# Weight splits of 1024 columns five steps ahead, and the decays moved beside the pair's own last projections, in a two-layer hybrid encoder on one Trainium2 core

## Chip, cores and metric

The kernel runs on one core of one Trainium2 chip. The metric is the device time of one execution in microseconds (us), median of several. Five engines work in their own queues, each strictly in order: PE (TensorE matmuls, with PEld for its weight loads), DVE (VectorE), ACT (ScalarE), POOL (GpSimd) and SP (SyncE, which here only issues transfers).

## What is computed

Two layers over 256 tokens of width 2048. Each projects the normalised input with one wide matrix, runs 16 heads of a bidirectional RWKV-7 scan beside 16 heads of windowed attention, gates both, and projects back onto the residual. Cut to what matters here:

```python
for l in range(DEPTH):
    h = rms_norm(x, norm_g[l])
    proj = jnp.einsum('btd,dc->btc', h, w_in[l])
    ...
    r, k, v, xw, xa = jnp.split(bidir_token_shift(rw_in, shift_mu[l]), rw_splits, axis=-1)
    y_rw = rwkv7_branch(r, k, v, xw, xa, ...)      # two scans, forward and backward
    y_at = window_attention(rope(q), rope(k_at), v_at, sink[l])
    mix = jnp.concatenate([y_rw * jax.nn.silu(g_rw), y_at * jax.nn.silu(g_at)], axis=-1)
    x = x + jnp.einsum('btc,cd->btd', mix, w_out[l])

# in rwkv7_branch, per direction d
w = -jax.nn.softplus(-(w0[d] + jnp.tanh(xw) @ decay_up[d])) - 0.5   # decays
a = jax.nn.sigmoid(a0[d] + xa @ iclr_up[d])                         # learning rates
```

`decay_up` and `iclr_up` have rank 96. With the row for w0, the decay tile has 97 rows.

## The kernel before

**Projections.** Every projection goes in column tiles of 128. A tile takes 16 steps (one per 128 rows of the contraction), and each step three matmuls of 256 columns (L286 to L288), since weights and inputs are held as a high and a low part: hi times XH, hi times XL, lo times XH. Weights come in halves of a tile, 128 x 1024, for 8 steps each: `wload` issues the transfer into raw (3 buffers), `wsplit` (L211) makes hi on ScalarE (L216) and lo = raw - hi on VectorE (L218), in two pieces of 512 columns, into rings of 2. A half's buffers are thus free again when PE has done the last step of the half before the one in progress. `Stream.run` walks the queue of all halves and lets the next half be loaded and split when `PREFETCH` = 2 steps of the present one are left.

**Windows.** The RWKV heads go in 8 pairs of heads per layer. After two tiles for xw and xa, pair p's four tiles (k, v, r and the gate gr, 16 steps each) fill window p: 64 steps in 14 slots of 4 or 5 steps. At the start of a slot the program puts small work of earlier pairs between the steps: `scan_p` of pair w-1 at the slots in STAGE_P (the elementwise preparation), `scan_i` of pairs w-2 and w-3 (inverts the in-chunk matrix, level by level: pq, QF, pd, tv, tt), `scan_b` of pairs w-3 and w-4 (walks the chunks: rh, suv, pcc, py). Windows 8 to 12 have the attention's projections and scores, then follow 16 tiles of the output projection. Windows 3 to 7 have all of this at once and are called steady here.

**Low-rank part.** At the first step of a pair's k tile `ups` issues two transfers into the ring g (2 buffers, L472): iup, 96 rows of 2 x 128, and dup, 97 rows of 2 x 128, for that pair. The ring g is shared with the gate's evacuation (`silu_evac`, L424 to L426), so SP can issue them only when the gate of the pair before is done (its last instruction writes vg). `value_evac` splits them into high and low parts after the v tile: iuh and duh on ScalarE (L455), iu and du on VectorE (L456), one buffer each. The first stage of `scan_p`, a window later, uses them in 12 matmuls (pza, L636 to L638), takes tanh of both halves (lw and th), and squares and scales k (t and kkr). The second adds 1 and runs two scans over lw. The third has the head sums of t (pk, L642), two exponentials and the reciprocal. The last sums km into pbn.

**Order.** PE runs in the order of the program. The other engines' instructions are ordered by a scheduler with priorities (lo gets 40, `scan_b` 95), so a split can run far from where it is written, as soon as the scheduler holds its operands for ready. PSUM pairs for the small work are a ring of 2.

Of the kernel before, what the change touches and what calls it, by code (L numbers as in the profile page):

```python
# [15 lines left out]
AF = mybir.ActivationFunctionType  # L16
# [5 lines left out]
T = 256  # L22
# [19 lines left out]


SLOTS = 14
STAGE_P = [4, 5, 6, 7, 8, 9, 10, 11, 13]
STAGE_I = (list(range(SLOTS)), [0, 1])
STAGE_B = (list(range(1, 14)), [1, 2, 3, 4])
ATT = [
# [3 lines left out]
]  # L52
PRIO_B = 95
PRIO_LO = 40
PREFETCH = 2


def _layout():
# [71 lines left out]
def hybrid_trunk_kernel(ctx, tc, xT, wi, wv, wo, par, fing, dup, iup, sink, pos, cst, out):  # L130
# [75 lines left out]
    def wload(src):  # L206
        raw = wrp.tile([128, 1024], F32, tag="raw", name="raw")
        SY.dma_start(out=raw, in_=src)
        return raw

    def wsplit(raw):  # L211
        hi = wsp.tile([128, 1024], F32R, tag="hi", name="hi")
        lo = wsp.tile([128, 1024], F32R, tag="lo", name="lo")
        for i in range(2):
            q = slice(i * 512, (i + 1) * 512)
            A.activation(hi[:, q], raw[:, q], AF.Copy)  # L216
            with tc.high_priority(offset=PRIO_LO):
                V.tensor_tensor(lo[:, q], raw[:, q], hi[:, q].bitcast(F32), op=ALU.subtract)  # L218
        return hi, lo

    def halves(src, first=None):
        return [lambda: wsplit(first if first is not None else wload(src[0])), lambda: wsplit(wload(src[1]))]

    class InTurn:

# [175 lines left out]
    def queue_inputs(l):  # L401
# [4 lines left out]
        def inproj(ct, evac, **kw):  # L406
            gemm(wi[l, ct], lambda: (L.XH, L.XL), evac, **kw)

        def shift_evac(j, place):
            def evac(pm):  # L410
                dst = place()
                u = st("u", [T], bufs=2)
                V.tensor_tensor(u, pm, L.norm.rb, op=ALU.mult)
                A.activation(dst, u, AF.Identity, scale=dpm(0, j))
                V.scalar_tensor_tensor(dst[:, 1:T], u[:, 0 : T - 1], prm(P_MU0, j), dst[:, 1:T], op0=ALU.mult, op1=ALU.add)
                V.scalar_tensor_tensor(dst[:, 0 : T - 1], u[:, 1:T], prm(P_MU1, j), dst[:, 0 : T - 1], op0=ALU.mult, op1=ALU.add)

            return evac
# [11 lines left out]
        def new(t, name, tag, bufs):  # L430
            def place():
                t[name] = st(tag, [T], bufs=bufs)
                return t[name]

            return place
# [37 lines left out]

            return begin

        def value_evac(p, t):
            ev = shift_evac(8 + p, new(t, "v", "vg", 8))

            def evac(pm):
                ev(pm)  # L480
                for n, rows in (("iu", RANK), ("du", RANK + 1)):
                    raw = t[n]
                    t[n] = (st(n + "h", [2, 128], F32R), st(n, [2, 128], F32R))
                    split(t[n], raw, rows)

            return evac

        for p, t in enumerate(L.ts):
            inproj(2 + 4 * p, shift_evac(p, new(t, "k", "kr", 4)), begin=ups(p, t))
            inproj(3 + 4 * p, value_evac(p, t))  # L490
            inproj(4 + 4 * p, shift_evac(16 + p, new(t, "r", "kr", 4)))
            inproj(5 + 4 * p, silu_evac(new(t, "gr", "vg", 8)))


# [125 lines left out]
    def layer(l):  # L620
# [22 lines left out]

        def scan_p(p, t):
            K, VV, R, iu, du = t["k"], t["v"], t["r"], t["iu"], t["du"]
            dd = lambda x: x.rearrange("p (d x) -> p d x", d=2)
            two = lambda x: x.unsqueeze(1).to_broadcast([128, 2, T])
            c8 = lambda x: x.rearrange("p (n j) -> p n j", j=64)  # L650

            pza = wpair("pza")
            pz, pa = pza[:, 0], pza[:, 1]
            for d in range(2):
                low_rank(pz[:, d * T : (d + 1) * T], [a[0 : RANK + 1, d, :] for a in du], [a[0 : RANK + 1] for a in L.TW])
            LW = st("lw", [2 * T])
            for d in range(2):
                low_rank(pa[:, d * T : (d + 1) * T], [a[0:RANK, d, :] for a in iu], [a[0:RANK] for a in L.XA])
            PA.activation(LW, pz, AF.Tanh, scale=0.5)
            TH = st("th", [2 * T])  # L660
            for d in range(2):
                PA.activation(TH[:, d * T : (d + 1) * T], pa[:, d * T : (d + 1) * T], AF.Tanh, scale=0.5, bias=dpm(NSH + 16, d * 8 + p))
            sq = st("t1", [T], bufs=3)
            PA.activation(sq, K, AF.Square, scale=prm(P_KK, p))
            KR = st("kkr", [T])
            PA.activation(KR, K, AF.Identity, scale=prm(P_KK, p))
            yield

            PV.tensor_scalar(LW, LW, 1.0, None, op0=ALU.add)
            msk = MSK.rearrange("p c j -> p (c j)")  # L670
            for x in (LW[:, 0:T], LW[:, T : 2 * T][:, ::-1]):
                PV.tensor_tensor_scan(x, msk, x, 0.0, op0=ALU.mult, op1=ALU.add)
            yield
            pk = wbank("pk")
            head_sums(pk, sq)
            PP = st("pp", [2, NC, 64])
            IP = st("ip", [2, NC, 64])
            PA.activation(PP.rearrange("p d c j -> p (d c j)"), LW, AF.Exp, scale=DECAY_C)
            PA.activation(IP.rearrange("p d c j -> p (d c j)"), LW, AF.Exp, scale=-DECAY_C)
            KD = st("kd", [T])  # L680
            PV.reciprocal(KD, pk[:, 0:T])
            PV.scalar_tensor_tensor(KD, KD, 1e24, KR, op0=ALU.min, op1=ALU.mult)
            yield

            MV = st("mv", [2, NC, 2, 64], bufs=3)
            BK = st("bk", [2, NC, 3, 64])
            km = st("lw", [2 * T])
            kr4 = KR.rearrange("p (c j) -> p c j", j=64)
            PV.scalar_tensor_tensor(MV[:, 0, :, 0, 1:64], PP[:, 0, :, 0:63], -1.0, kr4[:, :, 1:64], op0=ALU.mult, op1=ALU.mult)
            PV.scalar_tensor_tensor(MV[:, 1, :, 0, 0:63], PP[:, 1, :, 1:64], -1.0, kr4[:, :, 0:63], op0=ALU.mult, op1=ALU.mult)  # L690
            PA.activation(MV[:, 0, :, 0, 0:1], kr4[:, :, 0:1], AF.Copy, scale=-1.0)
            PA.activation(MV[:, 1, :, 0, 63:64], kr4[:, :, 63:64], AF.Copy, scale=-1.0)
# [261 lines left out]
        def scans(w):  # L954

            gens = []
            for lag, scan, at in ((4, scan_b, STAGE_B[1]), (3, scan_i, STAGE_I[1]), (3, scan_b, STAGE_B[0]), (2, scan_i, STAGE_I[0]), (1, scan_p, STAGE_P)):
                p = w - lag
                if 0 <= p < NP:
                    if (scan, p) not in chains:  # L960
                        chains[scan, p] = scan(p, L.ts[p])
                    gens.append((chains[scan, p], at))
            return gens
# [204 lines left out]
```

## Time and profile before

| | us |
|---|---|
| median of 3 runs | 1236.76 (1234.54 to 1237.37) |
| the profiled execution | 1234.27, span 1232.4 |
| PE busy | 1182.2 (96%) |
| VectorE busy | 930.7 (76%) |
| ScalarE busy | 743.0 (60%) |
| hi, 560 pieces of 512 | 328.1 busy, 625 ns each |
| lo, 560 pieces of 512 | 368.4 busy, 687 ns each |

The first part of the page gives each engine's busy time and share of the span. Group rows give line, engine, operation, output and inputs, shape and count, then busy time and mean, then the idle time of that engine just before and what ended it. A timeline row gives start, length, engine, line, operation, and in brackets the wait before it and its releaser. In a timeline an x2 row has merged two instructions.

### The profile page before, as it was taken

The page shows a single profiled execution, that of the slowest core. Times are in us where ns is not written, and L with a number is a line of the kernel's source. Part 1 is how long each engine was busy: PE and PEld are TensorE (multiplying, and loading weights), DVE is VectorE, ACT ScalarE, POOL GpSimd, SP SyncE. Part 2 cuts the span into 40 slices and gives each one's busy share as a digit, 9 for nine tenths or more (in the row PEclk, how much of TensorE's full clock was granted, in tenths as well). Part 3 has the DMA queues.
Part 4 walks back from the last instruction along what each step waited for, and adds up shares of the span by engine and source line. Part 5 has one row for each costly group of instructions (what it writes and reads, how often), then busy time and mean ns, then how long its engine had stood idle before and what let it go on. Part 6 is the DMA issues. An engine that isn't in the chain of part 4 may idle for free. (4 is left out here: it accounts for less than half of the span.)

```text
span 1232.4 us, 38183 instructions
## 1 busy us (share of the span) xinstructions
PE 1182.2 (96%) x16204; PEld 1096.3 (89%) x16204; DVE 930.7 (76%) x2067; ACT 743.0 (60%) x1838; POOL 19.1 (2%) x23
## 2 busy tenths in 40 slices
PE   6989999999999899999998999999999999999996
PEld 6978998999998889999998889999999888899996
DVE  7878778887876668856676788878887866786654
ACT  6546665766665567655555556675776565665553
POOL 0000000000000000000000000000000000000000
PEclk9999999999999999999999999999999999999998
DMA  7433333323323334467654333333323333445653
GB/s 249 157 136 116 105 117 109 105 96 114 119 89 99 117 112 144 140 214 240 209 182 147 124 128 93 106 111 111 105 94 106 124 102 127 131 130 178 211 192 121
DMA packets 60411, 166.72 MB, mean 135 GB/s; under 512 B 7728, under 2 KB 22736, under 8 KB 60240
## 3 DMA queue, kind: packets, MB, share of 16 engines
q1 hardware_dynamic: 60240, 164.27, 41.0%
q8 instruction: 127, 2.08, 0.7%
q14 instruction: 44, 0.36, 0.1%
HBM read 157.43 MB, written 4.19 MB: 131 GB/s over the span
## 5 line engine op out<-in xcount | busy, mean ns | idle before, releaser
L286 PE MATMUL pm<-XH,hi 128*128 128x256 f32 x1664 | 498.8, 300 | 9.4 <-ACT XH L179 5.9
L288 PE MATMUL pm<-XH,lo 128*128 128x256 f32 x1664 | 471.5, 283 | 4.8 <-DVE lo L218 4.6
L287 PE MATMUL pm<-XL,hi 128*128 128x256 f32 x1664 | 471.8, 284 | 0.1
L216 ACT ACTIVATE hi<-raw 128x512 fp32r<-128x512 f32 x560 | 328.1, 625 | 238.0 <-PE pm L287 147.9
L218 DVE TENSOR_TENSOR lo<-raw,hi 128x512 fp32r<-128x512 f32 x560 | 368.4, 687 | 96.7 <-ACT hi L216 89.2
L286 PEld LDWEIGHTS pm<-XH,hi 128*128 128x128 f32 x1664 | 317.3, 191 | 34.9 <-issue 13.0
L288 PEld LDWEIGHTS pm<-XH,lo 128*128 128x128 f32 x1664 | 318.3, 191 | 6.5 <-DVE lo L218 6.4
L287 PEld LDWEIGHTS pm<-XL,hi 128*128 128x128 f32 x1664 | 318.3, 191 | 0.9 <-DVE XL L180 0.9
L286 PE MATMUL pm<-MH,hi 128*128 128x256 f32 x512 | 144.1, 281 | 1.2 <-ACT hi L216 1.2
L288 PE MATMUL pm<-MH,lo 128*128 128x256 f32 x512 | 143.9, 281 | 0.4 <-DVE lo L218 0.4
L287 PE MATMUL pm<-ML,hi 128*128 128x256 f32 x512 | 143.8, 281 | 0.0
L286 PEld LDWEIGHTS pm<-MH,hi 128*128 128x128 f32 x512 | 96.6, 189 | 2.2 <-ACT hi L216 1.4
L288 PEld LDWEIGHTS pm<-MH,lo 128*128 128x128 f32 x512 | 96.6, 189 | 0.6 <-DVE lo L218 0.6
L287 PEld LDWEIGHTS pm<-ML,hi 128*128 128x128 f32 x512 | 96.6, 189 | 0.0
L908 ACT ACTIVATE suv<-pcc 64x128 f32<-64x128 f32 x128 | 34.2, 267 | 18.1 <-PE pq L835 11.8
L837 ACT ACTIVATE QF<-pq 128x256 f16<-128x256 f32 x80 | 30.8, 385 | 19.8 <-PE pq L835 19.0
L993 ACT ACTIVATE mv<-mv,mx 128x257 f32<-128x257 f32 x64 | 32.0, 503 | 17.5 <-DVE mx L990 17.3
L740 DVE TENSOR_TENSOR ge<-pg,C 128x1024 f32<-128x1024 f32 x32 | 39.1, 1221 | 3.2 <-PE pg L734 3.1
L844 DVE CAST_PREDICATED tv<-LV,pd 128x256 f16<-128x256 uint8 x80 | 34.4, 430 | 7.7 <-PE pd L843 6.9
L892 ACT ACTIVATE rh<-pcc 128x128 f32<-128x128 f32 x64 | 17.5, 273 | 35.4 <-PE pcc L890 35.0
L734 PE MATMUL pg<-mv,bk 64*128 64x128 f32 x512 | 37.2, 285 | 0.0
L845 DVE CAST_PREDICATED tt<-LV,pd 128x256 f16<-128x256 uint8 x80 | 34.1, 426 | 0.0
(239 smaller groups left out, 1845.8 us busy)
## 6 DMA issues: line engine op xcount, KB each, us to landing
raw<-wi SPq DMA_DIRECT2D x207, 512.0 KB, 3.3
raw<-wo SPq DMA_DIRECT2D x64, 512.0 KB, 4.3
raw<-wv SPq DMA_DIRECT2D x8, 512.0 KB, 3.3
rrot<-u SPq DMA_DIRECT2D x80, 32.0 KB, 2.0
vg<-xT SPq DMA_DIRECT2D x16, 128.0 KB, 4.6
xd<-vg SPq DMA_DIRECT2D x16, 128.0 KB, 2.4
vg<-xd SPq DMA_DIRECT2D x16, 128.0 KB, 3.3
g<-dup SPq DMA_DIRECT2D x16, 97.0 KB
```

The lines of the kernel that those rows point to most:

```text
L216: A.activation(hi[:, q], raw[:, q], AF.Copy)
L218: V.tensor_tensor(lo[:, q], raw[:, q], hi[:, q].bitcast(F32), op=ALU.subtract)
L286: PE.matmul(pm, wh, rh[:, kk, :], start=(kk == 0), stop=False)
L287: PE.matmul(pm, wh, rl[:, kk, :], start=False, stop=False)
L288: PE.matmul(pm, wl, rh[:, kk, :], start=False, stop=(kk == 15))
L734: PE.matmul(pg[:, h, c * 128 : (c + 1) * 128], BK[half[h], d, c, 1 - h : 3 - h, :].rearrange("p s j -> p (s j)"), MV[half[h], d, c].rearra ...
L740: V.tensor_tensor(GEd(d), pg.rearrange("p h (c x) -> p h c x", c=NC), gm[d].unsqueeze(1).unsqueeze(1).to_broadcast([128, 2, NC, 128]), op= ...
L837: A.activation(t_sub(QF), flat4(pq[:, :, 0:128]), AF.Copy)
L844: V.copy_predicated(t_sub(TC), t_mask, flat4(pd[:, :, 0:128]))
L845: V.copy_predicated(v_sub(TT), v_mask, flat4(pd[:, 0, 128:384].rearrange("p (d x) -> p d x", d=2)))
L908: A.activation(here(h), pc[half[h], 1], AF.Copy)
L993: A.activation(Sc[:, h, q, 0:257], Sc[:, h, q, 0:257], AF.Exp, scale=0.125, bias=mx[:, q : q + 1], accum_out=den[:, q : q + 1])
```

## The change

It does four things. (1) A weight half is split in one instruction of 1024 columns per engine (only the very first half keeps two pieces). (2) `PREFETCH` goes from 2 to 5. (3) The low-rank part of `scan_p` (12 matmuls, both tanh, the +1 and the two scans over lw) becomes `scan_d`, at slots 12 and 13 of the pair's own window; `scan_p` keeps nine stages, at slots 3 to 11 instead of 4 to 11 and 13. (4) The split of iup's and dup's tiles is written after the r tile instead of the v tile.

```diff
-STAGE_P = [4, 5, 6, 7, 8, 9, 10, 11, 13]
+STAGE_D = [12, 13]
+STAGE_P = [3, 4, 5, 6, 7, 8, 9, 10, 11]
...
-PREFETCH = 2
+PREFETCH = 5
...
-    def wsplit(raw):
+    def wsplit(raw, parts=1):
...
-        for i in range(2):
-            q = slice(i * 512, (i + 1) * 512)
+        for i in range(parts):
+            q = slice(i * 1024 // parts, (i + 1) * 1024 // parts)
             A.activation(hi[:, q], raw[:, q], AF.Copy)
...
-        return [lambda: wsplit(first if first is not None else wload(src[0])), lambda: wsplit(wload(src[1]))]
+        return [lambda: wsplit(first, 2) if first is not None else wsplit(wload(src[0])), lambda: wsplit(wload(src[1]))]
...
-        def value_evac(p, t):
-            ev = shift_evac(8 + p, new(t, "v", "vg", 8))
+        def receptance_evac(p, t):
+            ev = shift_evac(16 + p, new(t, "r", "kr", 4))
...
-            inproj(3 + 4 * p, value_evac(p, t))
-            inproj(4 + 4 * p, shift_evac(16 + p, new(t, "r", "kr", 4)))
+            inproj(3 + 4 * p, shift_evac(8 + p, new(t, "v", "vg", 8)))
+            inproj(4 + 4 * p, receptance_evac(p, t))
...
-        def scan_p(p, t):
-            K, VV, R, iu, du = t["k"], t["v"], t["r"], t["iu"], t["du"]
+        def scan_d(p, t):
+
+            iu, du = t["iu"], t["du"]
             pza = wpair("pza")
...
+            t.update(LW=LW, TH=TH)
+            yield
+
+            PV.tensor_scalar(LW, LW, 1.0, None, op0=ALU.add)
+            msk = MSK.rearrange("p c j -> p (c j)")
+            for x in (LW[:, 0:T], LW[:, T : 2 * T][:, ::-1]):
+                PV.tensor_tensor_scan(x, msk, x, 0.0, op0=ALU.mult, op1=ALU.add)
+            yield
+
+        def scan_p(p, t):
+            K, VV, R, LW, TH = t["k"], t["v"], t["r"], t["LW"], t["TH"]
...
-            for lag, scan, at in ((4, scan_b, STAGE_B[1]), (3, scan_i, STAGE_I[1]), (3, scan_b, STAGE_B[0]), (2, scan_i, STAGE_I[0]), (1, scan_p, STAGE_P)):
+            for lag, scan, at in ((4, scan_b, STAGE_B[1]), (3, scan_i, STAGE_I[1]), (3, scan_b, STAGE_B[0]), (2, scan_i, STAGE_I[0]), (1, scan_p, STAGE_P), (0, scan_d, STAGE_D)):
```

The order on the engines, at three places. In brackets stands what an instruction waits for: DMAHW is a transfer, PE, Activation (ScalarE) and DVE are engines. Lines of the changed kernel are 1 to 8 higher than those of before (L455 is L456 there, L890's rh is L900, L908 is L916).

ScalarE in window 6, from the copy of AB to the first tanh; duh and iuh (the high parts of dup's and iup's tiles for pair 6) are the third and second row from the end. Before:

```order
L231 ACTIVATE AB<-ge 64x512
L770 ACTIVATE bt<-pt 128x768 [waits PE_49]
L775 ACTIVATE suv<-pt 64x4x64 x4
L231 ACTIVATE MH<-t_4473 128x256
L216 ACTIVATE hi<-raw 128x512 [waits DMAHW0_49,PE_49,Activation_49]
L216 ACTIVATE hi<-raw 128x512
L414 ACTIVATE kr<-u,DP 128x256 [waits DVE_49]
L892 ACTIVATE rh<-pcc 128x128 [waits PE_49]
L837 ACTIVATE QF<-pq 128x2x64x2 [waits PE_49]
L455 ACTIVATE duh<-g 97x256 [waits DMAHW3_49,PE_49]
L455 ACTIVATE iuh<-g 96x256 [waits DMAHW2_49,PE_49]
L231 ACTIVATE lw<-pza 128x512 [waits PE_49]
```

The same window of the changed kernel, from the silu's tanh (g<-g) on:

```order
L426 ACTIVATE g<-g 128x256 [waits DVE_49]
L866 ACTIVATE q_4352<-pf 128x512 [waits PE_49]
L950 ACTIVATE t_4396<-py,PR 128x256 [waits PE_49]
L878 ACTIVATE vf<-pn 128x512 [waits PE_49]
L900 ACTIVATE rh<-pcc 128x128 [waits PE_49]
L456 ACTIVATE iuh<-g 96x256 [waits DMAHW2_49]
L456 ACTIVATE duh<-g 97x256 [waits DMAHW3_49]
L217 ACTIVATE hi<-raw 128x1024 [waits DMAHW7_49,PE_49,Activation_49]
L916 ACTIVATE suv<-pcc 64x2x64 [waits PE_49]
L916 ACTIVATE suv<-pcc 64x2x64
L232 ACTIVATE MH<-t_4396 128x256 [waits DVE_49]
L232 ACTIVATE AB<-ge 64x512 x2
```

The two splits moved from behind the second rh of the window to behind the first, ahead of suv, MH and AB, and no longer wait for PE.

VectorE at the start of the same window, from the gate's last instruction (vg) to the next lo; ge is the masked in-chunk matrix that AB is copied from, t the finished output of pair 2, whose high part is MH. Before:

```order
L426 SCALAR_TENSOR_TENSOR vg<-g 128x256 [waits Activation_49]
L804 COPY tv<-EYE 128x512 [waits PE_49]
L740 TENSOR_TENSOR ge<-pg,C 128x2x512 [waits PE_49]
L231 TENSOR_TENSOR t_4473<-t_4473,bv 128x256 [waits Activation_49]
L804 COPY tt<-EYE 128x512 [waits PE_49]
L231 SCALAR_TENSOR_TENSOR t_4473<-t_4473,vg 128x256 [waits DVE_49]
L740 TENSOR_TENSOR ge<-pg,C 128x2x512 [waits PE_49]
L218 TENSOR_TENSOR lo<-raw,hi 128x512 [waits DMAHW7_49,PE_49,Activation_49]
```

The changed kernel, from the gate's first instruction (g<-pm):

```order
L425 TENSOR_TENSOR g<-pm,rb 128x256 [waits PE_49]
L232 SCALAR_TENSOR_TENSOR lw<-MSK,lw 128x256 [waits DVE_49]
L232 SCALAR_TENSOR_TENSOR lw<-MSK,lw 128x256
L219 TENSOR_TENSOR lo<-raw,hi 128x1024 [waits DMAHW6_49,Activation_49]
L427 SCALAR_TENSOR_TENSOR vg<-g 128x256 [waits Activation_49]
L812 COPY tv<-EYE 128x512 [waits PE_49]
L748 TENSOR_TENSOR ge<-pg,C 128x2x512 [waits PE_49]
L812 COPY tt<-EYE 128x512 [waits PE_49]
L457 TENSOR_TENSOR iu<-g,iuh 96x256 [waits DMAHW2_49,Activation_49]
L457 TENSOR_TENSOR du<-g,duh 97x256 [waits DMAHW3_49,Activation_49]
L748 TENSOR_TENSOR ge<-pg,C 128x2x512 [waits PE_49]
L232 TENSOR_TENSOR t_4396<-t_4396,bv 128x256
```

The two scans over lw now stand between the gate's instructions, and iu and du ahead of the second ge and of t.

ScalarE in window 1 of the first layer, around t and kkr (k squared and k scaled, for pk). Before:

```order
L414 ACTIVATE kr<-u,DP 128x256 [waits DVE_49]
L455 ACTIVATE duh<-g 97x256 [waits DMAHW1_49,PE_49]
L455 ACTIVATE iuh<-g 96x256 [waits DMAHW0_49,PE_49]
L231 ACTIVATE lw<-pza 128x512 [waits PE_49]
L231 ACTIVATE th<-pza,DP 128x256 x2
L231 ACTIVATE t_789<-kr,PR 128x256
L231 ACTIVATE kkr<-kr,PR 128x256
```

The changed kernel:

```order
L426 ACTIVATE g<-g 128x256 [waits DVE_49]
L217 ACTIVATE hi<-raw 128x1024 [waits DMAHW5_49,PE_49,Activation_49]
L232 ACTIVATE t_742<-kr,PR 128x256
L232 ACTIVATE kkr<-kr,PR 128x256
L217 ACTIVATE hi<-raw 128x1024 [waits DMAHW6_49,DVE_49,PE_49]
L415 ACTIVATE kr<-u,DP 128x256 [waits DVE_49]
L232 ACTIVATE pp<-lw 128x512
L232 ACTIVATE ip<-lw 128x512
```

The splits and the tanh no longer stand ahead of t; in this window iuh and duh come ten rows behind t. SP's order is the same in both kernels at these places.

More of the change, by code (lines that the diff above doesn't have):

```diff
@@ L642, in head_sums @@
                 PE.matmul(o[r, 0:T], bones[r, r], x[r, 0:T], start=True, stop=True)
-        def scan_p(p, t):
-            K, VV, R, iu, du = t["k"], t["v"], t["r"], t["iu"], t["du"]
-            dd = lambda x: x.rearrange("p (d x) -> p d x", d=2)
-            two = lambda x: x.unsqueeze(1).to_broadcast([128, 2, T])
-            c8 = lambda x: x.rearrange("p (n j) -> p n j", j=64)
+        def scan_d(p, t):
+            iu, du = t["iu"], t["du"]
             pza = wpair("pza")
@@ L655, in scan_p @@
                 low_rank(pz[:, d * T : (d + 1) * T], [a[0 : RANK + 1, d, :] for a in du], [a[0 : RANK + 1] for a in L.TW])
-            LW = st("lw", [2 * T])
             for d in range(2):
                 low_rank(pa[:, d * T : (d + 1) * T], [a[0:RANK, d, :] for a in iu], [a[0:RANK] for a in L.XA])
+            LW = st("lw", [2 * T])
             PA.activation(LW, pz, AF.Tanh, scale=0.5)
@@ L662, in scan_p @@
                 PA.activation(TH[:, d * T : (d + 1) * T], pa[:, d * T : (d + 1) * T], AF.Tanh, scale=0.5, bias=dpm(NSH + 16, d * 8 + p))
[L663 to L666, printed above, removed]
+            t.update(LW=LW, TH=TH)
             yield
@@ L673, in scan_p @@
             yield
-            pk = wbank("pk")
-            head_sums(pk, sq)
+        def scan_p(p, t):
+            K, VV, R, LW, TH = t["k"], t["v"], t["r"], t["LW"], t["TH"]
+            dd = lambda x: x.rearrange("p (d x) -> p d x", d=2)
+            two = lambda x: x.unsqueeze(1).to_broadcast([128, 2, T])
+            c8 = lambda x: x.rearrange("p (n j) -> p n j", j=64)
+            sq = st("t1", [T], bufs=3)
+            PA.activation(sq, K, AF.Square, scale=prm(P_KK, p))
+            KR = st("kkr", [T])
+            PA.activation(KR, K, AF.Identity, scale=prm(P_KK, p))
+            yield
             PP = st("pp", [2, NC, 64])
@@ L679, in scan_p @@
             PA.activation(IP.rearrange("p d c j -> p (d c j)"), LW, AF.Exp, scale=-DECAY_C)
+            yield
+            pk = wbank("pk")
+            head_sums(pk, sq)
             KD = st("kd", [T])
```

## The prediction

> **What bounds the kernel now.** I read the page first, then one steady window, the waits, and the timelines where a wait looked odd.
>
> ```profile
> span 1232.4 us, 38183 instructions
> PE 1182.2 (96%) x16204; PEld 1096.3 (89%) x16204; DVE 930.7 (76%) x2067; ACT 743.0 (60%) x1838; POOL 19.1 (2%) x23
> ...
> L216 ACT ACTIVATE hi<-raw 128x512 fp32r<-128x512 f32 x560 | 328.1, 625 | 238.0 <-PE pm L287 147.9
> L218 DVE TENSOR_TENSOR lo<-raw,hi 128x512 fp32r<-128x512 f32 x560 | 368.4, 687 | 96.7 <-ACT hi L216 89.2
> ```
>
> ```profile
> 249.90:291.90 42.00, 42.00 (x755) 38.13 (x754) 35.42 (x74) 27.83 (x73) 1.01 (x1) 1.00 0.33 107
> ```
>
> TensorE is busy for 1182.2 of 1232.4 us, and in a steady window (columns: length, then busy time of PE, PEld, DVE, ACT, POOL, granted clock) for all 42.00 us. The change does not touch the number of matmuls, so time can only come from the 50 us in which PE idles, and go into new idling. DVE and ACT have slack, but they run their queues in order: what matters is what stands in front of the thing that PE waits for. The view of the waits names them:
>
> ```profile
> ACT duh L455 <- DMA g<-dup: 17.4, 4, 4.6
> ...
> PE pbn L642 <- DVE lw L231: 5.6, 2, 2.8
> PE pk L642 <- ACT t L231: 5.4, 2, 2.9
> ```
>
> Columns: us in total, times, longest. The first line is the odd one: four times ScalarE sat over 4 us at the split of dup's tile, waiting for its transfer. Issue (SP's queue) and end of that wait (ScalarE's timeline), four pairs, with iup beside one:
>
> ```profile
> 19.40 0.34 SPq L472 DMA_DIRECT2D g<-dup  x1
> 59.07 0.30 SPq L472 DMA_DIRECT2D g<-dup  x1
> 539.47 0.42 SPq L472 DMA_DIRECT2D g<-iup  x1
> 539.94 0.30 SPq L472 DMA_DIRECT2D g<-dup  x1
> 658.42 0.30 SPq L472 DMA_DIRECT2D g<-dup  x1
> ```
>
> ```profile
> 28.08 0.42 ACT L455 ACTIVATE duh<-g 97x256 fp32r<-97x256 f32 x1 [4.59 <-DMA g<-dup]
> 66.70 0.42 ACT L455 ACTIVATE duh<-g 97x256 fp32r<-97x256 f32 x1 [4.38 <-DMA g<-dup]
> 542.47 0.40 ACT L455 ACTIVATE iuh<-g 96x256 fp32r<-96x256 f32 x1
> 547.38 0.42 ACT L455 ACTIVATE duh<-g 97x256 fp32r<-97x256 f32 x1 [4.50 <-DMA g<-dup]
> 666.69 0.42 ACT L455 ACTIVATE duh<-g 97x256 fp32r<-97x256 f32 x1 [3.94 <-DMA g<-dup]
> ```
>
> From issue to use: 8.68, 7.63, 7.44 and 8.27 us, mean 8.0. iup, of about the same size, was used 3.00 us after its issue without a wait. The second case cost PE directly:
>
> ```profile
> 69.07 0.65 PE L642 MATMUL pk<-t,C 64*64 64x256 f32 x4 [2.92 <-ACT t L231]
> ```
>
> The operand t stands behind duh in ScalarE's queue. Elsewhere the split comes later than that, held back by the low-rank matmuls of the pair before, and sees nothing of the transfer; in the steady window used below dup goes out at 252.77:
>
> ```profile
> 264.60 0.42 ACT L455 ACTIVATE duh<-g 97x256 fp32r<-97x256 f32 x1
> ```
>
> **Part 1: the low-rank split loses its cover.** This carries the forecast. The order of the changed kernel has, in windows 3 to 7 of both layers, iuh and duh right behind the first rh of the window, and the matmuls that held them back now run in the window before. So ScalarE meets dup's transfer in 10 windows. The steady window of before, which starts near 249.9 us:
>
> ```profile
> 252.77 0.30 SPq L472 DMA_DIRECT2D g<-dup  x1
> ```
>
> ```profile
> 254.82 0.28 ACT L892 ACTIVATE rh<-pcc 128x128 f32<-128x128 f32 x1
> ...
> 258.01 0.54 ACT L908 ACTIVATE suv<-pcc 64x128 f32<-64x128 f32 x2
> 258.57 1.28 ACT L231 ACTIVATE AB<-ge 64x512 f16<-64x512 f32 x2
> ...
> 262.28 0.42 ACT L231 ACTIVATE MH<-t 128x256 fp32r<-128x256 f32 x1
> ```
>
> ```profile
> 250.05 0.42 DVE L424 TENSOR_TENSOR g<-pm,rb 128x256 f32<-128x256 f32 x1 [0.18 <-PE pm L288]
> 250.60 1.29 DVE L218 TENSOR_TENSOR lo<-raw,hi 128x512 fp32r<-128x512 f32 x2
> 251.81 0.42 DVE L426 SCALAR_TENSOR_TENSOR vg<-g 128x256 f32<-128x256 f32 x1
> ...
> 254.48 0.43 DVE L231 TENSOR_TENSOR t<-t,bv 128x256 f32<-128x256 f32 x1 [0.92 <-ACT t L942]
> ...
> 255.02 0.42 DVE L231 SCALAR_TENSOR_TENSOR t<-t,vg 128x256 f32<-128x256 f32 x1
> 255.40 1.23 DVE L740 TENSOR_TENSOR ge<-pg,C 128x1024 f32<-128x1024 f32 x1
> ```
>
> ```profile
> 260.00 0.45 PE L913 MATMUL pcc<-suv,bt 128*64 128x64 f32 x8
> ...
> 260.61 0.33 PE L825 MATMUL pq<-tv,AB 64*64 64x32 f16 x10
> ```
>
> Two durations more, ScalarE's and VectorE's:
>
> ```profile
> 15.78 1.04 ACT L1065 ACTIVATE mv<-X 128x1024 f32<-128x1024 f32 x1
> ```
>
> ```profile
> L231 DVE TENSOR_TENSOR_SCAN lw<-MSK,lw 128x256 f32<-128x256 f16 x32 | 20.4, 679 | 0.5
> L456 DVE TENSOR_TENSOR du<-g,duh 97x256 fp32r<-97x256 f32 x16 | 6.7, 418 | 11.7 <-ACT duh L455 11.7
> ```
>
> SP may issue dup only after VectorE's vg, since they share the ring g. In the changed order the two scans (0.68 each, some 0.1 of each overlapped) and one lo of 1.2 for two halves (1.29) stand before vg, so vg ends about 1.1 later and dup goes out at 253.9. It lands 8.0 later: duh starts at 261.9, ScalarE having reached it at 255.1. From there two chains. ScalarE: duh 0.42, the whole hi 1.04, suv 0.54 ends 263.9; L913 is due at 260.00, so PE waits 3.9. VectorE, which waits in order as well: du 0.42, ge 1.23, t 0.43 and 0.42 ends 264.8; then ScalarE's MH 0.42 and AB 1.28 end 266.5. L825 is due at 260.61: 5.9 us in all, the first 3.9 inside it. In window 3 there is no t and no MH yet: AB runs 263.9 to 265.2, 4.6 us. Sum: 8 x 5.9 + 2 x 4.6 = **56.4 us**. Queued behind the wait are a weight half (needed only at step 16, behind L825) and bt, suv, kr, which follow PE's own delay and add nothing. Bounds per window: landing 7.44 to 8.68, and dup's issue 0 to 1.1 later, 4.2 to 6.6 us; over ten windows, less 1.3 twice, 40 to 63.
>
> [...]
>
> **Part 2: the clock.** The same step (L286, one matmul a step) behind the gap at 69 us, in two stretches of 3.41 us (columns: PE, PEld, granted clock):
>
> ```profile
> 70.51:73.92 3.41, 2.28 (x6) 1.67 (x6) 0.50 0.00 0
> 73.92:77.33 3.41, 2.65 (x11) 1.83 (x10) 1.00 0.82 268
> ```
>
> 6 steps against 11: a half-clock stretch costs 5/11 of 3.41, 1.55 us. One gap of 2.92 had it, so I put one behind each of the ten longer gaps: **15.5 us**, between none and two each, 0 to 31.
>
> [...]
>
> **Part 3: what it removes.** In window 1, t no longer stands behind duh or the tanh, which moved to window 0: both pk waits go, 5.4 us, and a half-clock stretch behind each (the second taken like the first), 3.1: **-8.5 us**. pbn there keeps its 2.8 a layer: between pk and pbn lies one slot less than before, but VectorE's chain starts on time. It may go altogether or grow by 4.
>
> **Part 4: one split of 1024.** 279 splits save ScalarE 1.15 - 1.04 (hi x2 below) and VectorE 1.29 - 1.23 each, beside PE, worth nothing. The risk is lateness: lo now needs the whole hi. In the output stage a buffer comes free once a half tile:
>
> ```profile
> 574.82 1.15 ACT L216 ACTIVATE hi<-raw 128x512 fp32r<-128x512 f32 x2 [1.65 <-PE pm L287]
> ...
> 577.71 1.15 ACT L216 ACTIVATE hi<-raw 128x512 fp32r<-128x512 f32 x2 [1.03 <-issue]
> ```
>
> 2.89 us for 1.04 + 1.23 = 2.27: it fits with 0.6 to spare, so nothing; five steps ahead helps only where a buffer is already free. Without that cover up to 0.6 us a tile. I keep 5 us either way for these, for pbn in steady windows and for the attention windows, whose waits I can't follow.
>
> **Sum.** The profiled execution took 1234.27 us (span 1232.4), the median is 1236.76. 56.4 + 15.5 - 8.5 = 63.4 more: 1297.7 for that execution, **1300 us** on the median.
>
> **Rivals.** (a) *Covered after all, faster.* Only pk is won: 1236.8 - 8.5 = 1228. From duh's start to AB's end are 4.6 us, so PE sees nothing if duh starts by 256.0, that is if dup lands within 2.1 us of 253.9, or if the splits ran at their written place behind r. Against it: four landings over 7.4, iup's 3.00, and the compiled order. Chance 0.07. (b) *dup lands like iup*, 3.0: duh at 256.9, AB at 261.5, 0.9 us a window and no half clock: 1236.8 + 9 - 8.5 = 1237. Against it the same rows; 0.03. (c) *PE's own slack takes half*, L913 and L825 being due later because other work delays PE: about 3 us a window, few stretches: 1236.8 + 30 + 5 - 8.5 = 1263; against it the 42.00 busy us; 0.10. (d) *Weights late too*: the 0.6 spare fails in the 64 output half tiles or so, up to 38 us more, 1300 + 25 = 1325; 0.05. The forecast keeps 0.75.
>
> Range: the low corner is 40 us of stalls, no half clock, -14 if pbn goes as well: 1263, and rival (c) lies there; 1258 allows the 5 us. The high corner with 63 and 31 is 1322. Together they leave (a), (b) and half of (d) out. A measurement of this kernel can tell 0.2%, 2.5 us, from no change: faster 0.07, same 0.03, slower 0.90.
>
> **What would show it.** Right: ScalarE waits for g<-dup in ten more places, 6 to 7 us each; L913 and L825 late by 4 and 2 more; windows 3 to 7 about 48 to 50 us instead of 42; more stretches at 0.50; no pk wait. Wrong: windows 3 to 7 still 42 us, or long waits at lo in the output stage.

## The result, and the profile after

The changed kernel takes **1313.11 us** (median of 4 runs, 1312.2 to 1313.97) against 1236.79 for the kernel before (4 runs beside it, 1234.54 to 1237.37): ratio 1.0621, 95% interval 1.0602 to 1.0639. It is 76.3 us slower; 63 were forecast. The page of the profile first (columns of the groups: busy time, mean ns, then the engine's idle time just before and what ended it):

```profile
span 1312.2 us, 37629 instructions
PE 1211.5 (92%) x16204; PEld 1119.0 (85%) x16204; DVE 908.8 (69%) x1788; ACT 725.6 (55%) x1561; POOL 19.6 (1%) x23
...
L219 DVE TENSOR_TENSOR lo<-raw,hi 128x1024 fp32r<-128x1024 f32 (+1 forms) x281 | 342.2, 1218 | 135.7 <-ACT hi L217 134.2
L217 ACT ACTIVATE hi<-raw 128x1024 fp32r<-128x1024 f32 (+1 forms) x281 | 296.2, 1054 | 211.3 <-PE pm L288 163.5
...
L457 DVE TENSOR_TENSOR du<-g,duh 97x256 fp32r<-97x256 f32 x16 | 6.8, 424 | 49.8 <-ACT duh L456 49.8
```

The wide splits did what they are for: VectorE has 22 us less to do and ScalarE 17. TensorE executes the same 16,204 matmuls; it idles 101 us instead of 50 (span less busy time), and is busy 29 us longer with the same work, since part of it ran at a lower clock (0.963 on the mean, 0.990 before). VectorE idles 49.8 us for one row, du, which stands behind dup's transfer. The waits of the changed kernel (us in total, times, longest):

```profile
ACT duh L456 <- DMA g<-dup: 51.2, 13, 4.7
...
ACT iuh L456 <- DMA g<-iup: 30.7, 13, 5.4
PE pcc L921 <- ACT suv L916: 29.4, 10, 3.3
...
PE pq L833 <- ACT AB L232: 12.7, 19, 1.3
...
PE pbn L643 <- DVE lw L232: 5.2, 2, 3.4
```

Thirteen waits for dup instead of four, and ten new waits of TensorE on suv, one for each steady window. Both pk waits are gone. Window 6 of the first layer now, from dup's issue on SP to what ScalarE does behind it:

```profile
280.87 0.30 SPq L473 DMA_DIRECT2D g<-dup  x1
```

```profile
281.82 0.28 ACT L900 ACTIVATE rh<-pcc 128x128 f32<-128x128 f32 x1
283.83 0.42 ACT L456 ACTIVATE iuh<-g 96x256 fp32r<-96x256 f32 x1 [1.74 <-DMA g<-iup]
288.86 0.42 ACT L456 ACTIVATE duh<-g 97x256 fp32r<-97x256 f32 x1 [4.61 <-DMA g<-dup]
289.19 1.04 ACT L217 ACTIVATE hi<-raw 128x1024 fp32r<-128x1024 f32 x1
290.13 0.54 ACT L916 ACTIVATE suv<-pcc 64x128 f32<-64x128 f32 x2
291.70 0.42 ACT L232 ACTIVATE MH<-t 128x256 fp32r<-128x256 f32 x1 [1.03 <-DVE t L232]
292.02 1.26 ACT L232 ACTIVATE AB<-ge 64x512 f16<-64x512 f32 x2
```

From issue to use dup takes 7.99 us. Behind it stand hi, suv, MH and AB, as the order said. TensorE in the same stretch:

```profile
290.72 0.70 PE L921 MATMUL pcc<-suv,bt 128*64 128x64 f32 x8 [3.16 <-ACT suv L916]
292.69 0.23 PE L833 MATMUL pq<-tv,AB 64*64 64x32 f16 x1 [0.84 <-ACT AB L232]
293.34 0.45 PE L833 MATMUL pq<-tv,AB 64*64 64x32 f16 x10 [0.42 <-ACT AB L232]
```

And the window as a whole (columns as before: length, PE, PEld, DVE, ACT, POOL, granted clock), with three stretches of the clock, the first of which begins 0.8 us before the stall ends:

```profile
276.89:326.00 49.11, 44.23 (x756) 39.96 (x754) 34.54 (x67) 27.70 (x65) 1.01 (x1) 0.93 0.27 92
289.93:293.34 3.41, 1.36 (x19) 1.07 (x19) 2.86 (x5) 2.32 (x7) 0.00 (x0) 0.50 0.00 0
293.34:296.76 3.42, 3.42 (x30) 3.33 (x31) 1.82 (x6) 3.35 (x8) 0.00 (x0) 0.50 0.48 158
296.76:300.17 3.41, 3.41 (x72) 3.05 (x73) 2.54 (x5) 2.79 (x6) 0.00 (x0) 1.00 0.11 22
```

42.00 us became 49.11, and two stretches of half clock come with the stall. Worked out from the start of each window's first matmul, both layers together, the profiled executions compare like this (us; "rest" is the xw and xa tiles, windows 8 to 12 and the output projection; the labels are those of the experiments below; window 7, in which more small work stands, takes 64.8 us before, windows 3 to 6 41.6 to 42.0):

| | windows 0 to 2 | windows 3 to 7 | rest | median |
|---|---|---|---|---|
| before | 193.3 | 464.8 | 554.9 | 1236.8 |
| changed | 196.9 | 535.8 | 560.0 | 1313.1 |
| e1_rows96 | 194.4 | 486.2 | 555.0 | 1257.8 |
| e2_in_turn | 199.0 | 480.2 | 556.4 | 1256.9 |
| e5_before_rows96 | 183.0 | 465.2 | 551.8 | 1222.0 |
| e6_in_turn_narrow | 190.9 | 473.7 | 548.2 | 1236.1 |
| e10_keep_busy3 | 197.8 | 531.6 | 557.1 | 1308.7 |
| e11_in_turn_1024 | 196.6 | 479.8 | 559.9 | 1255.2 |
| e12_in_turn_five | 200.0 | 474.4 | 555.4 | 1246.2 |

71 of the 76 us arose in windows 3 to 7. The time columns but the last are of one execution each; that of e12_in_turn_five was 4.7 us above its median.

### The profile page after: what moved, and what is told of

Read it like the earlier page. It is cut to its first block, busy times and chain, and to the rows that moved or that the text cites. A ratio compares the mean times of both kernels' runs of the same rounds, so it can differ in the third digit from the quotient of the medians.

```text
span 1312.2 us, 37629 instructions
## 1 busy us (share of the span) xinstructions
PE 1211.5 (92%) x16204; PEld 1119.0 (85%) x16204; DVE 908.8 (69%) x1788; ACT 725.6 (55%) x1561; POOL 19.6 (1%) x23
## 5 line engine op out<-in xcount | busy, mean ns | idle before, releaser
L287 PE MATMUL pm<-XH,hi 128*128 128x256 f32 x1664 | 506.2, 304 | 9.9 <-ACT XH L180 6.1
L289 PE MATMUL pm<-XH,lo 128*128 128x256 f32 x1664 | 477.9, 287 | 8.4 <-DVE lo L219 8.4
L219 DVE TENSOR_TENSOR lo<-raw,hi 128x1024 fp32r<-128x1024 f32 (+1 forms) x281 | 342.2, 1218 | 135.7 <-ACT hi L217 134.2
L217 ACT ACTIVATE hi<-raw 128x1024 fp32r<-128x1024 f32 (+1 forms) x281 | 296.2, 1054 | 211.3 <-PE pm L288 163.5
L287 PEld LDWEIGHTS pm<-XH,hi 128*128 128x128 f32 x1664 | 323.7, 195 | 36.3 <-issue 13.2
L289 PEld LDWEIGHTS pm<-XH,lo 128*128 128x128 f32 x1664 | 324.2, 195 | 11.1 <-DVE lo L219 11.0
L288 PEld LDWEIGHTS pm<-XL,hi 128*128 128x128 f32 x1664 | 324.8, 195 | 0.9 <-DVE XL L181 0.9
L916 ACT ACTIVATE suv<-pcc 64x128 f32<-64x128 f32 x128 | 34.5, 270 | 41.4 <-PE pq L843 22.0
L921 PE MATMUL pcc<-suv,bt 128*64 128x64 f32 x384 | 22.9, 244 | 29.4 <-ACT suv L916 29.4
L921 PEld LDWEIGHTS pcc<-suv,bt 128*64 128x64 f32 x384 | 16.0, 145 | 36.5 <-ACT suv L916 31.4
L457 DVE TENSOR_TENSOR du<-g,duh 97x256 fp32r<-97x256 f32 x16 | 6.8, 424 | 49.8 <-ACT duh L456 49.8
```

The lines of the kernel that those rows point to most:

```text
L287: PE.matmul(pm, wh, rh[:, kk, :], start=(kk == 0), stop=False)
L288: PE.matmul(pm, wh, rl[:, kk, :], start=False, stop=False)
L289: PE.matmul(pm, wl, rh[:, kk, :], start=False, stop=(kk == 15))
L916: A.activation(here(h), pc[half[h], 1], AF.Copy)
L921: PE.matmul(pS[half[h], d, :], BT[:, h, d, i, :], SUV[:, d, ci[d], h, :], start=(i == 0), stop=True, skip_group_check=True)
```

## The experiments

The theory was the forecast's: in the new order the low-rank splits stand in front of suv and AB in ScalarE's queue and wait there for dup, whose single transfer takes 8.0 us from issue to use, against 3.00 for iup's 96 rows, because of its 97 rows (theory A). Rivals: the move of the decays costs by itself, or the wide splits do, or the half clock does most of it.

**e1_rows96**: the order stays, dup lands sooner.

```diff
-SY.dma_start(out=t[n][0:rows], in_=src[l, :, :, p * 128 : (p + 1) * 128].rearrange("d r c -> r d c"))
+s3 = src[l, :, :, p * 128 : (p + 1) * 128].rearrange("d r c -> r d c")
+SY.dma_start(out=t[n][0:RANK], in_=s3[0:RANK])
+if rows > RANK:
+    SY.dma_start(out=t[n][RANK:rows], in_=s3[RANK:rows])
```

> The changed kernel with dup's tile loaded in two transfers, rows 0 to 95 and row 96, and nothing else changed: iuh and duh stand at the same place behind rh. [...] Theory B (the windows are longer because splits of 1024 come late or because VectorE's order got worse, and the wait at dup only fills time that PE loses anyway): little comes back, 1300 us or more.

Measured: 1257.79 us (1256.58 to 1260.07), ratio to before 1.0194 (1.0159 to 1.0229). One transfer cut in two gives back 55 us. Its waits, then issue and use of dup in window 6:

```profile
ACT iuh L456 <- DMA g<-iup: 30.5, 13, 4.8
...
ACT duh L456 <- DMA g<-dup: 1.3, 1, 1.3
```

```profile
264.62 0.44 SPq L474 DMA_DIRECT2D g<-dup  x1
265.11 0.58 SPq L476 DMA_DIRECT2D g<-dup  x1
```

```profile
269.31 0.42 ACT L456 ACTIVATE duh<-g 97x256 fp32r<-97x256 f32 x1 [1.34 <-DMA g<-dup]
```

The same 97 rows are there 4.7 us after the first issue instead of 8.0, and of thirteen waits one is left. But 21 us over the kernel before remain. The time is near what theory A gives, 1253 to 1257 us by an estimate in which each of the ten windows gets back 5.6 to 6 of its 7.1 us; the windows are not: windows 3 to 7 still lose 1.0 to 3.9 us where 1.1 to 1.5 would be left, ScalarE still stands at iup (30.5 us), and two stretches at half clock are left.

**e9_rows89**: the same cut at row 89. It tells "97 is a bad number of rows" from "any cut helps".

```diff
-SY.dma_start(out=t[n][0:RANK], in_=s3[0:RANK])
+c = rows if rows == RANK else 89
+SY.dma_start(out=t[n][0:c], in_=s3[0:c])
...
```

> As e1_rows96, the changed kernel with dup's 97 rows loaded in two transfers, but of 89 rows and of 8 in place of 96 and 1. [...] Rival B (any cut of the 97 rows helps, since a single transfer of that many rows or bytes is the slow thing): like e1, 1253 to 1262.

Measured: 1309.06 us (2 runs), ratio 1.0604 (1.0546 to 1.0662).

```profile
278.22 0.31 SPq L475 DMA_DIRECT2D g<-dup  x1
```

```profile
286.00 0.42 ACT L456 ACTIVATE duh<-g 97x256 fp32r<-97x256 f32 x1 [3.33 <-DMA g<-dup]
```

89 rows take 7.8 us like 97 (8.0), and the time stays. So neither the cut nor the number of bytes matters (iup's 96 rows, one less than dup's, were used 3.00 us after issue in the kernel before), but the row count. Why the count does it is not shown; as dup's or iup's transfer, only 89, 96 and 97 rows were tried, and the remainders of 8 and 1. In the trace's packet records of the changed kernel, the 386 packets of 512 bytes of one iup and one dup run from 282.49 to 288.33, in e1_rows96 from 266.33 to 268.78, at 27 to 29 ns each. In the changed kernel the first 192 of them, as many as iup has, start within 0.8 us (282.49 to 283.28); the 194 behind them, as many as dup has, start one after the other over 4.9 us (283.40 to 288.30), one every 25 ns.

**e2_in_turn**: dup's transfer as in the changed kernel, but the splits of iup and dup keep their written place on ScalarE and VectorE, behind the r tile.

```diff
-split(t[n], raw, rows)
+hi, lo = (a[0:rows] for a in t[n])
+PA.activation(hi, raw[0:rows], AF.Copy)
+PV.tensor_tensor(lo, raw[0:rows], hi.bitcast(F32), op=ALU.subtract)
```

> [...] Theory A: no wait at a transfer in any steady window, all ten fall back to about 42 us: 1313 - 71 = 1242, and perhaps 3 less from window 2, 1236 to 1244. Theory B: 1300 us or more. New risk for both: the 12 pza matmuls at slot 12 now follow the split closely; up to 1 us a window more.

Measured: 1256.86 us (1256.18 to 1259.56), ratio 1.0185 (1.0156 to 1.0214). No wait for dup is left, and 56.2 us of the 76.3 go. The size of what is left was not expected (1236 to 1244): both ways of removing the wait end 20 us above before, so something else in the change costs 20 us.

**e3_move_only** and **e4_split_only**: the change cut in halves, first the changed kernel with the old weight splits (`PREFETCH = 2`, two pieces), then the kernel before with the new ones (`PREFETCH = 5`, one piece).

> The changed kernel with PREFETCH 2 and the split in two pieces of 512 as before, so only the low-rank part is moved. Theory A: the move alone carries the loss, 1300 to 1330 us; iuh and duh stand even two rows further ahead here, in front of rh, so perhaps a few us more than with the whole change. Theory B: without the splits of 1024 most of the loss is gone, 1245 us or less.

> The kernel before with only PREFETCH 5 and one split of 1024 per half; the low-rank part stays where it was. Theory A: this half of the change costs and gains next to nothing, 1228 to 1242 us. Theory B: 1270 us or more.

Measured: 1295.75 us (1293.6 to 1299.2), ratio 1.0498 (1.0465 to 1.0531), and 1241.12 us (1238.41 to 1243.15), ratio 1.005 (1.0035 to 1.0066). e3_move_only ended 4 us under the range of theory A. The move brings the stall by itself, with iuh and duh here in front of rh rather than behind it; the waits of e3_move_only:

```profile
ACT duh L456 <- DMA g<-dup: 63.8, 15, 5.0
...
PE pcc L911 <- ACT rh L900: 36.1, 11, 3.8
```

In the old order the wide splits cost 0.5%. In the new one they add 17 us (from e3_move_only to the changed kernel).

**e6_in_turn_narrow**, **e11_in_turn_1024**, **e12_in_turn_five**: which part leaves the 20 us. All three are e2_in_turn, which has no wait for dup, with the old weight splits put back: e6 has both old values, e11 keeps the new width alone, e12 the new distance alone.

```diff
 # e6
-PREFETCH = 5
+PREFETCH = 2
-    def wsplit(raw, parts=1):
+    def wsplit(raw, parts=2):
 # e11: only PREFETCH = 2; e12: only parts=2
```

> The changed kernel with the low-rank splits issued in the written order (behind the receptance tile) as in e2_in_turn, and besides with weight splits in two pieces and two steps ahead as before the change. So only the move of the decays and learning rates to the window before is left, without its wait for dup. It tells where the 20 us come from that e2_in_turn keeps over the kernel before. Theory A (they come from the wide split: VectorE's lo of 1.2 us stands in front of the small operations ge, tv and tt that TensorE waits for, in the moved order): 1236 to 1244 us, windows 3 to 7 at 42.0 to 42.4 us. Rival B (they come from the move itself, whatever the width of the split): 1250 to 1260, windows 3 to 7 still about 43.8.

> e2_in_turn (1256.9 us) with the weight splits two steps ahead in place of five, still in one piece of 1024 columns. e2 and e6_in_turn_narrow (1236.1) differ by 20.8 us in two things, the width and the steps ahead; this and e12 tell which. Theory A (width: one lo of 1.2 us in VectorE's queue in place of two of 0.65, in front of the tv that TensorE waits for): 1250 to 1260 us, windows 3 to 7 at 43.6 to 44. Rival B (steps ahead: weight splits that stand earlier in the queues of ScalarE and VectorE, in front of what is urgent): 1234 to 1241, windows about 43.2.

> e2_in_turn (1256.9 us) with the weight splits in two pieces of 512 columns, still five steps ahead; the counterpart of e11. Theory A (width): 1234 to 1241 us, windows 3 to 7 about 43.2. Rival B (steps ahead): 1250 to 1260, windows 43.6 to 44. If both lie between, the two add up.

Measured: e6 1236.09 us (ratio 1.0012, 0.9996 to 1.0029), e11 1255.22 (1.0166, 1.0138 to 1.0195), e12 1246.23 (1.0085, 1.0054 to 1.0115). So the new splits cost 20.8 us in this order, the width alone 19, the distance alone 10; the two don't add up. Window 6 of e2, e6, e11 and e12:

```profile
259.42:303.25 43.83, 42.33 (x756) 38.08 (x754) 34.60 (x67) 27.53 (x65) 1.01 (x1) 1.00 0.31 103
```

```profile
253.01:296.20 43.19, 42.13 (x756) 38.09 (x754) 35.19 (x75) 28.37 (x73) 1.01 (x1) 1.00 0.32 104
```

```profile
257.61:301.42 43.81, 42.32 (x755) 38.08 (x754) 34.60 (x67) 27.39 (x65) 1.01 (x1) 1.00 0.30 103
```

```profile
258.40:301.68 43.28, 42.33 (x756) 38.19 (x754) 35.27 (x75) 28.35 (x73) 1.01 (x1) 1.00 0.32 104
```

In these windows it is the width: 43.8 with it, 43.2 to 43.3 without. e6 came out at the time that theory A expected, but not with the windows (42.0 to 42.4): 1.2 us in each of windows 4 to 6 are the move's. One place where e2 loses is TensorE's wait for tv; VectorE of e2, then of e6:

```profile
283.74 1.22 DVE L219 TENSOR_TENSOR lo<-raw,hi 128x1024 fp32r<-128x1024 f32 x1
284.87 0.48 DVE L416 SCALAR_TENSOR_TENSOR vg<-u,PR,vg 128x255 f32<-128x255 f32 x1
285.27 0.43 DVE L854 CAST_PREDICATED tv<-LV,pd 128x256 f16<-128x256 uint8 x1
```

```profile
276.98 0.68 DVE L219 TENSOR_TENSOR lo<-raw,hi 128x512 fp32r<-128x512 f32 x1
277.58 0.44 DVE L854 CAST_PREDICATED tv<-LV,pd 128x256 f16<-128x256 uint8 x1
```

A lo of 1.22 us and a vg stand in front of tv instead of one of 0.68, and in e2 TensorE waits for it:

```profile
285.75 0.30 PE L845 MATMUL pq<-tv,AB 64*64 64x32 f16 x16 [0.68 <-DVE tv L854]
```

That this is the width alone is not shown: in e12, where two pieces of lo and the vg stand in front of tv, TensorE waits there too (0.49 us). All its waits over 0.15 us in window 6 add up to 1.39 us in e2, 1.37 in e11, 0.80 in e12 and 0.94 in e6.

In the table, 6.5 us between e2 and e6 lie in windows 3 to 7, 8 in windows 0 to 2, and 8 in the rest; in e12's execution most of the loss lies in the last two. The view of the waits says what TensorE waited for, in the whole execution of e2 and of e6: for tv 9.3 and 3.5 us, for lo 8.5 and 4.1, for tt (written by VectorE too) 5.6 and 2.7, for hi 4.0 and 1.9. No experiment takes these one by one.

**e5_before_rows96**: the kernel before with dup in 96 rows and 1 (the diff of e1_rows96).

> The kernel before with one edit: dup's 97 rows come in two transfers, of 96 rows and of 1. Order and everything else as before. Theory A (the four waits for dup in the kernel before are the cause of its pk waits, and dup's length is due to its 97 rows): no ScalarE wait for dup over 1.5 us is left, both pk waits (5.4 us) and the half-clock stretches behind them (3.1) go, and 2 us in the output stage of the first layer: 1236.8 - 5.4 - 3.1 - 2 = 1226 us, 1223 to 1231. Rival B (pk waits for other things as well, or the second transfer costs SP and the ring as much as it saves): 1234 to 1239, pk still named among the waits.

Measured: **1221.99 us** (1220.85 to 1223.83), ratio 0.9895 (0.9873 to 0.9918), the fastest of all and 1 us under the range of theory A. No wait of TensorE for pk is left, and window 1 of the two layers is 8.8 us shorter. Against this kernel, which has no wait for dup either, e6_in_turn_narrow shows what the move costs by itself: 14 us. Its view of the waits has what e5 lacks: TensorE waits 4.8 us for ge (12 times), 2.7 for tt in front of pq (8 times) and 1.7 for du in front of pza, which now stands close behind its split.

**e7_keep_busy**, **e8_keep_busy2**, **e10_keep_busy3**: what the half clock costs. In each steady window of the changed kernel, matmuls are added on TensorE in front of the one that waits for suv.

```diff
+if i == 0 and p < 5:
+    for d in [0, 1] * 9:                   # e10: * 11
+        for h in range(2):                 # e7: into pc[half[h], 0, d, :]
+            PE.matmul(pyt[half[h], T : T + 64], t["VF"][half[h], d, cs(ci[d])], RH[half[h], d, :], start=True, stop=True)
 if i < NC - 1:
     for d in range(2):
         for h in range(2):
             PE.matmul(pS[half[h], d, :], BT[:, h, d, i, :], ...)
...
 # e10 besides: the same with * 5 behind the py matmuls of that stage
```

> The changed kernel with 36 matmuls of 64x64 added on TensorE in each of the ten windows with a stall, right in front of the matmul that waits for suv (the changed kernel's L921). They repeat an earlier product into a place that is overwritten later, so results don't change, and every engine's order is otherwise the same. They fill some 2.6 to 3.2 us of TensorE's idle 3.2 us and leave the waits as they are. Theory A (the half clock follows TensorE's idling and is a cost on top of the stall, two stretches of 1.55 us a window): no 0.50 stretch in windows 3 to 7, those windows about 46 us in place of 49, and 1313 - 31 = 1282 us, 1276 to 1292. Rival B (the half clock comes from something else, such as the load before it or the time of the window, or costs nothing because other work bounds the steps behind it): 1308 to 1318, 0.50 stretches still there or the windows still about 49 us. If only one stretch of two goes: about 1298.

> As e7_keep_busy, the changed kernel with 36 matmuls of 64x64 added in front of the matmul that waits for suv in each of the ten windows, but into a bank that no pending operation reads. In e7 they wrote beside what suv reads, so they came to wait for suv themselves and ran behind the stall. Here they have no wait of their own: they took 2.31 us in e7 and run inside the stall, which leaves some 0.9 of its 3.2 us idle; the waits of ScalarE and VectorE, and the two short ones of TensorE behind (0.84 and 0.42), stay. Theory A (the half clock follows TensorE's idling in a stretch of 3.41 us; in the runs so far it came after idling of 1.9 us and more in one stretch and never after less than 1.4): no 0.50 stretch in windows 3 to 7, those windows about 46 us, 1313 - 31 = 1282 us, 1276 to 1290. Rival B (the half clock comes with the waits, not with idling, or the work behind the stall would not be faster at full clock): 1308 to 1318.

> As e8_keep_busy2, with 44 matmuls in place of 36 in front of the matmul that waits for suv, and 20 more behind it, in front of the one that waits for AB. e8 left one 0.50 stretch in most of the ten windows, because the wait for AB grew to 1.28 us and came together with 0.9 us of the first stall; and its windows stayed at 49.0 us because the stretch that went lay ahead of AB, where TensorE waits anyway, and the one that stayed lay behind AB, where each step counts. Here both waits are filled to about 0.4 us each. Theory A (a stretch behind AB costs 5/11 of 3.41 us, 1.55 a window, and is caused by idling): no 0.50 stretch in windows 3 to 7, windows 47.5 us, 1313 - 15.5 = 1297 us, 1291 to 1302. Rival B (a half clock costs nothing here even behind AB, since other work paces the steps): 1309 to 1317 with no 0.50 stretch left. If the fillers do not remove the stretches, nothing follows.

Measured: 1315.48 us, 1313.25 us and 1308.66 us (1306.46 to 1310.64; ratio 1.0598, 1.0561 to 1.0634). In e10_keep_busy3 the 20 added matmuls behind change part of what py collects, so its output differs; all other work and its order are the changed kernel's. In e7 the edit missed: the added matmuls waited for suv themselves and ran behind the stall, so nothing follows from its time alone.

```profile
292.19 2.31 PE L921 MATMUL pcc<-rh,vf 64*64 64x64 f32 x72 [3.03 <-ACT suv L916]
```

In e8 they filled the stall, but the wait for AB grew from 0.84 to 1.28 and most windows kept one stretch at half clock:

```profile
283.02 2.31 PE L921 MATMUL py<-rh,vf 64*64 64x64 f32 x72
286.32 0.45 PE L925 MATMUL pcc<-suv,bt 128*64 128x64 f32 x8 [0.98 <-ACT suv L916]
...
288.29 0.20 PE L833 MATMUL pq<-tv,AB 64*64 64x32 f16 x1 [1.28 <-ACT AB L232]
```

In e10 no stretch at half clock is left in windows 3 to 7. Its window 6, and a place further down in it:

```profile
275.36:324.49 49.13, 47.01 (x883) 42.25 (x882) 34.49 (x67) 27.59 (x65) 1.01 (x1) 1.00 0.28 92
```

```profile
307.48 0.30 PE L843 MATMUL pq<-tv,AB 64*64 64x32 f16 x16 [0.71 <-DVE tv L852]
```

Full clock, and 49.13 us all the same: the half clock costs 4 us in all (1313.1 to 1308.7; in windows 3 to 7 of the two profiled executions 535.8 to 531.6), not 15.5, and theory A's range is missed. What decides is named in the second row. ScalarE and VectorE of the changed kernel ahead of the same matmuls:

```profile
296.52 1.04 ACT L217 ACTIVATE hi<-raw 128x1024 fp32r<-128x1024 f32 x1
297.59 1.23 DVE L219 TENSOR_TENSOR lo<-raw,hi 128x1024 fp32r<-128x1024 f32 x1 [0.92 <-ACT hi L217]
...
304.66 1.22 DVE L219 TENSOR_TENSOR lo<-raw,hi 128x1024 fp32r<-128x1024 f32 x1
305.80 0.75 DVE L232 SCALAR_TENSOR_TENSOR mv<-pp,kkr 128x252 f32<-128x252 f32 x2
306.57 0.42 DVE L414 TENSOR_TENSOR u<-pm,rb 128x256 f32<-128x256 f32 x1
306.93 1.23 DVE L219 TENSOR_TENSOR lo<-raw,hi 128x1024 fp32r<-128x1024 f32 x1
308.07 0.48 DVE L416 SCALAR_TENSOR_TENSOR vg<-u,PR,vg 128x255 f32<-128x255 f32 x1
308.46 0.43 DVE L852 CAST_PREDICATED tv<-LV,pd 128x256 f16<-128x256 uint8 x1
```

From AB at 292.02 on ScalarE works off, without a wait, what dup held up, and so reaches this hi only 18.0 us into the window, counted from its first step (12.3 in e2); VectorE's lo waits for it, and from that lo to tv VectorE has no wait either, 10.9 us. In e10 the clock does not move this: hi starts 18.1 us into the window, and lo to tv are 10.8 us. The start of a step, counted from the window's first, shows the hand-over (us; in brackets the difference from before):

```
step   before   changed         e10             e2              e6
 13      9.45   15.39 (+5.94)   15.26 (+5.81)    9.96 (+0.51)    9.83 (+0.38)
 18     13.56   19.23 (+5.67)   17.85 (+4.30)   12.54 (-1.02)   12.40 (-1.15)
 36     24.95   30.74 (+5.79)   30.71 (+5.76)   24.91 (-0.03)   23.91 (-1.04)
 64     42.01   49.11 (+7.10)   49.13 (+7.12)   43.83 (+1.81)   43.19 (+1.18)
```

By step 18, e10 has won 1.4 us over the changed kernel, which runs at half clock there. By step 36 it is gone: e10 has waited 0.71 us for tv, which the changed kernel, late by its clock, reaches just as it is done (written until 308.89, used from 308.96).

## Why the prediction was right, and where not

The forecast of 1300 us, slower, held: measured were 1313.1. The chain e2, e6, before takes the 76.3 us apart: 56.2 are the wait for iup and dup (changed to e2), 20.8 the new splits (e2 to e6), -0.7 the move without its wait (e6 to before). These runs were not made side by side, and the kernel before had medians from 1234.2 to 1236.8 beside them, so each term is good to some 3 us; beside its own runs of before, e6 is 1.4 us slower, with no change inside its interval. The forecast had 71.9 (56.4 and 15.5), 0 and -8.5.

**Part 1, the split loses its cover: right, mechanism and size.** ScalarE waits for dup in the ten windows, dup lands 7.99 us behind its issue (8.0 taken), TensorE's L921 and L833 are late. Step 13 is 5.4 us later than in e2_in_turn (15.39 against 9.96), where 5.9 were forecast. dup goes out 3.98 us behind the window's reference point (280.87 less 276.89), 4.0 were taken. Two signs came out smaller than told: ScalarE stands 4.6 us at dup, not 6 to 7, because it stood 1.74 at iup just before; and TensorE's waits make 3.16 + 0.84 + 0.42 us, the rest of the 5.4 being matmuls between them at half clock. All in all 56.2 us, of which about 4 are the half clock; 56.4 were forecast without it. Rival (b), that dup lands like iup, is out as a forecast; e1 made it true, and the price put on it, 1237, was missed by 21 us. Step 13 of e1's window 6 is 0.9 us later than before in the second layer, as that rival had it, and 2.6 in the first; the rest arises further on in the windows, as in e2, and no run with dup in two transfers and narrow splits says how much of it is part 4. Rival (a), priced at 1228, was missed for the reasons under parts 3 and 4: with the splits at their written place e2 takes 1256.9. Of rival (d), weights late as well, the size was near (25 against 20.8) but not the place.

**Part 2, the clock: the step that failed.** Its count was too low (two stretches for each stall, not one) and its price too high. "A half-clock stretch costs 5/11 of 3.41" was read from steps that TensorE paced alone. Here the first stretch lies around TensorE's own waits, and the loss of the second was taken back at step 36, where VectorE's tv, behind ScalarE's late hi, is late anyway. e10 shows 4 us for all of them, where 15.5 were forecast.

**Part 3, what it removes: right, but not all of it.** Both pk waits went, as forecast; e5 finds 8.8 us in window 1 against 8.5. What failed is the silent assumption that the move costs nothing else: e6 against e5 says 14 us. In the profiled executions 8.5 of them lie in windows 3 to 7 (window 6 ends 1.2 us late) and 7.9 in windows 0 to 2, less 3.6 in the rest. The waits for ge, tt and du named under e5 come to 9.2 us in the whole execution; none was taken away by itself. The wait for pbn kept its size as forecast (5.2 us for both layers, 5.6 before).

**Part 4, the split of 1024: failed.** "Worth nothing", 5 us either way, was argued from the output stage and from busy time. The cost was 20.8 us in the moved order (6 in the old one). The forecast had looked at lateness of lo itself, and in one place. The runs show in its place that TensorE waits 8.7 us more for tv and tt, which queue behind other work on VectorE, and 4.4 more for lo, most of it in the attention windows (5.8 us in e2, 2.0 in e6). The output stage, the place that was named, has 3 us of it (184.3 us in both layers in e2, 181.1 in e6). That an instruction of 1.2 us can't be passed on an in-order engine fits the width's 19 us, but is argued: the order of the queue changed with the width, and five steps ahead cost 10 us without it.

The parts that failed cancel in part: 15.7 too much for wait and clock, 20.8 and 7.8 too little for splits and move, 13 us in sum. That 1313 came so near 1300 is to that extent luck; that the wait for dup carries the loss is not.

## What to carry to other kernels

Before moving an instruction that waits for a transfer, look up what it now stands in front of on its in-order engine, and take the transfer's time from the trace; four rare waits in the profile before gave the price of ten new ones. Count rows: 97 in one transfer cost 8.0 us, 96 and 1 in two cost 4.7, and this edit alone, on the kernel before, gave 1.05%. And a delay put into a pipeline is worth what the latest queue makes of it: filling a stall and restoring the clock won 4 us at most while ScalarE and VectorE had their backlog to work off.

## What the runs showed of the hardware

**Rows in a transfer.** From issue to use, 97 rows in one transfer took 8.0 us and 89 rows 7.8 (e9); 96 rows and 1 in two transfers took 4.7 (e1), and iup's 96 rows in one 3.00 (before). In the changed kernel's window 6 the 192 packets of iup start within 0.8 us, the 194 of dup within 4.9.

**The clock.** In the traces of the kernel before and of the changed kernel the half clock (0.50) comes and goes on a grid of 3.41 us: the first three that begin in the changed kernel, at 16.86, 57.82 and 81.72 us, are 12 and 7 steps of it apart. TensorE's idle time was added up in each stretch of the grid, past the first 7 us of the execution. Stretches at full clock with one at 0.50 behind them had 1.48 to 2.71 us of idling in the kernel before and 1.89 to 3.07 in the changed one; those with another at full clock behind them had at most 1.47 and 1.56. A stretch at 0.50 had another at 0.50 behind it where it had 0.45 us of idling or more, and one at full clock where it had 0.17 or less. So the stalls of 3.16 us here, with the short waits behind them, brought two stretches each (6.83 us at 0.50 in all ten windows), where a gap of 2.92 alone had brought one before (3.41 us). Once 1.48 us of idling, less than half a stretch, went before a half clock.
